# HGRN2's values and K turned by VectorE in 32x32 blocks and moved within SBUF, with the state products 25 steps later

## The chip, the cores and the metric

The kernel runs on one core of one Trainium2 chip. The metric is the device time of one execution in microseconds, the median of several runs; smaller is better. All times below come from those runs and from one execution recorded by the hardware profiler.

## The reference, cut to what matters

One inference step of one decoder layer for two groups of requests that share all weights: a prompt of 16 learned tokens and 256 tokens, and 8 samples of one token each, 280 columns in all. The layer is a half-step feed-forward network, a mixer, and a second feed-forward network, each with a layer norm. The mixer projects x to ten parts of 2048 columns and runs two recurrences beside each other, retention (8 heads of 256) and HGRN2 (16 heads of 128). The change is in HGRN2:

```
f = lb + (1.0 - lb) * sigmoid(f_h)          # forget gate, per channel
k = 1.0 - f
q = silu(q_h);  v = i_h
# per chunk, b = cumsum(log f):
o     = (A * v summed over j <= i) + (q * exp(b)) @ S
S_new = exp(b_last) * S + einsum('bhjd,bhjv->bhdv', k * exp(b_last - b), v)
```

The last line sums over the tokens j. On the chip the projections leave channels on the partitions and tokens along the row, so for this sum both the decayed K and v must be turned, so that tokens lie on the partitions. Outputs are the layer's result for both groups and the new states of both recurrences.

## The kernel before

**Products and weights.** Every projection runs in three passes on TensorE (PE), with weights and activations each split into a high and a low part (`dense`, L202; the products are L218). Weights come in units of eight 128x128 blocks. Each unit is loaded by a DMA on SP's queue (`raw`, L185), cast by ScalarE (ACT) to the high part (`whi`, L188), and VectorE (DVE) subtracts that for the low part (`wlo`, L189). Each of the three has three buffers, so the load of unit n+3 waits until `wlo` of unit n is made, and `whi` of unit n+3 waits until PE is through with unit n. 

**Groups.** The projection to ten parts is worked in groups of two outputs of 128 channels: for each unit u (a pair of HGRN2 heads and a retention head, 8 units) the groups f, q_h, i_h, q_r, k_r, v_r, then four gate groups of the unit before. In unit 0, f and q_h are one group, and so are i_h and q_r. A group has 16 k-steps, each of them six products (two weight blocks in three passes), so a steady unit has 160 k-steps. A group's two outputs take two of the four PSUM banks of the pool `ps_a`; the next group takes the other two, if they are free. The function `evacuate` (L643 on) reads them: f by a sigmoid and a scaling on ACT (L653, L654) and k = 1 - f (L655); q_h by a sigmoid on ACT (L660) and a multiplication on DVE (recorded at the helper's line L240); i_h by two ACT copies to v (L667, L668); q_r and k_r by the rotation on DVE (L677 to L680); v_r by ACT copies to the same tile v (L684, L686). The tiles f, k, v and vth have one buffer each.

**The mixers run between the k-steps.** `mix_hg` (HGRN2) and `mix_ret` (retention) are generators: after each k-step of a projection `pump` lets each run on to its next `yield n`, where n is the number of k-steps to wait. PE's order is the program's order. The orders on the other engines are made by the framework's scheduler before the run and are fixed as well; each engine works strictly in its order, and so does SP's queue of DMA issues.

**HGRN2's steps that the change touches.** Early in `mix_hg`, PE turns v by two transposes for each head (L875), ACT copies them to `vth` (L879), and POOL copies v's first and last tokens to `ends` (L750, L751). After the scan of decays, `turned(h)` turns K by two transposes for each head (L982) with an ACT copy to `kth` (L983). Later come the state products `pst` (km by vm for the learned tokens at L1022, then kth by vth at L1024), an ACT copy and two DVE steps to `Sh` (L1027), and its DMA out (L1030). After these, the samples' products `pq` (L1039) and the outputs follow. `load(1)` and `values(1)` fetch the second head's sample states; each first touches the tile by a small POOL copy of something that must be done before.

Unit 0 begins before the steady rhythm, unit 1 with other spacings; units 2 to 7 are called steady.

Of the kernel before, what the change touches and what calls it, by code (L numbers as in the profile page):

```python
# [18 lines left out]
P = 128  # L19
# [4 lines left out]
NMETA, SEQ, NS = 16, 256, 8  # L24
# [104 lines left out]
def trunk(ctx: ExitStack, tc: tile.TileContext, A, O):  # L129
# [417 lines left out]
    with tc.tile_pool(name="yp", bufs=1) as yp:  # L547
# [7 lines left out]
        with tc.tile_pool(name="mp", bufs=1) as mp:  # L555
# [73 lines left out]
            def project(groups):  # L629
                for grp in groups:  # L630

                    bank = mx_bank if grp[0] == (QKV_ORDER[2], 0) else acc_bank
                    outs = [bank(f"pj_{n}{c}") for n, c in grp]
                    x0s = [NMETA if n in LIVE else 0 for n, _ in grp]
                    if grp[0] == (QKV_ORDER[0], 0):
                        outs = norm1.first(block, outs, x0s)
                    elif grp[0] == (QKV_ORDER[2], 0):
                        v = st["i_h"] = tmp("v", (P, 2, T))
                        outs = norm1.second(block, outs, x0s, (v[:, 0, :], v[:, 1, :]))
# [71 lines left out]

            NB2 = LP - 2 * P
# [8 lines left out]
            def upper_upper_lower(out, x, at=0):  # L721
                n = x.shape[0]
                nc.scalar.copy(out[:n], x)
# [22 lines left out]
            def mix_hg(u, f, k, q, v):  # L746

                calm = 2
                ends = tmp("ends", (P, 2, 2, NMETA))
                nc.gpsimd.tensor_copy(ends[:, :, 0, :], v[:, :, :NMETA])  # L750
                nc.gpsimd.tensor_copy(ends[:, :, 1, :], v[:, :, T - NMETA :])  # L751
# [117 lines left out]
                vt = tmp("vth", (P, 2, 2, P))  # L869
                vrow = []  # L870
                for h in range(2):

                    pt = mx_bank("pt")
                    for b in range(2):
                        nc.tensor.transpose(pt[:, b * P : (b + 1) * P], v[:, h, NMETA + b * P : NMETA + (b + 1) * P], ident)  # L875
                    x = pt[:64, 2 * P : 3 * P]
                    if h:
                        nc.tensor.transpose(x, ends.rearrange("p c a t -> p (c a t)"), ident)
                    nc.scalar.copy(vt[:, h], pt[:, : 2 * P].rearrange("p (b f) -> p b f", b=2))  # L879
                    if h:  # L880
# [93 lines left out]
                kts = []  # L974

                def turned(h):
                    kt = tmp("kth", (P, 2, P), bufs=2)
                    kts.append(kt)
                    pt = mx_bank("ptk")
                    for b in range(2):  # L980
                        t0 = NMETA + b * P
                        nc.tensor.transpose(pt[:, b * P : (b + 1) * P], K[:, h, t0 : t0 + P], ident)  # L982
                    nc.scalar.copy(kt, pt[:, : 2 * P].rearrange("p (b f) -> p b f", b=2))  # L983
# [20 lines left out]
                turned(0)  # L1004
                load(1)
                yield 4
                turned(1)
# [5 lines left out]
                if u != 1:  # L1013
                    samples(1)
                    yield 4 if u == 0 else 5

                Ss = []
                for h in range(2):
# [4 lines left out]
                    for b in range(2):  # L1023
                        nc.tensor.matmul(pst[:, (b + 1) * P : (b + 2) * P], kts[h][:, b, :], vt[:, h, b, :], start=True, stop=True)  # L1024
# [9 lines left out]
                yield (8, 11, 45)[min(u, 2)]  # L1034
# [342 lines left out]
```

## Time and profile before

| what | value |
|---|---|
| device time, median of 3 runs | 2566.84 us |
| lowest and highest run | 2566.56 and 2567.51 us |
| span of the profiled execution | 2563.9 us |
| instructions in it | 56275 |
| VectorE, ScalarE busy | 66%, 54% |
| granted TensorE clock | nine tenths or more in all 40 slices |
| packets on the hardware DMA queue q1 | 156352 |

The span runs from the first to the last recorded instruction. No device time is listed for the profiled execution apart from the runs; its span lies 2.9 us below their median. The page also cuts the span into 40 equal slices of 64 us. The digit of each is the busy share in tenths: VectorE stands at 4 to 6 in the feed-forward networks and at 7 to 9 in the slices of the mixer, from about 770 us to 1850 us, and the DMA share alternates there between 6 and 7.

In rows of the timeline the first number is the start, the second the duration, then engine, line, operation, output and inputs. A bracket at a row's end says how long the engine stood idle before it, and what ended the wait.

### The profile page before, as it was taken

What the parts mean: (1) busy time and instruction counts of PE and PEld (TensorE: products, weight loads), DVE (VectorE), ACT (ScalarE), POOL (GpSimd) and SP (SyncE); (2) the same over time, 40 slices, a digit from 0 to 9 for tenths busy, and PEclk for the clock granted to TensorE, in tenths of its full rate; (3) what the DMA queues carried; (4) which work ended last, traced back from release to release, by engine and by line L of the source; (5) the groups of instructions that cost most, each with busy time, mean ns of one, the idle gap of its engine ahead of it and who ended that gap; (6) DMA issues with size and microseconds to landing.
All of it is one profiled execution on the core that took longest, in us unless ns stands there. A gap on an engine that the chain in (4) does not pass through costs nothing.

```text
span 2563.9 us, 56275 instructions
## 1 busy us (share of the span) xinstructions
PE 2553.4 (100%) x23424; PEld 2534.4 (99%) x23424; DVE 1702.8 (66%) x2827; ACT 1392.2 (54%) x2186; POOL 57.0 (2%) x152
## 2 busy tenths in 40 slices
PE   9999999999999999999999999999999999999999
PEld 9999999999999999999999999999999999999998
DVE  6444544475569878777777777777885555556555
ACT  5444444444456767767676666675564444444443
POOL 0000000000000000000000000000000000000000
PEclk9999999999999999999999999999999999999999
DMA  7555555555555876767676767675556565565554
GB/s 244 183 187 183 187 182 184 186 182 186 184 201 180 287 265 232 264 214 260 212 264 215 259 223 255 224 239 188 196 190 197 194 197 195 194 196 195 195 195 149
DMA packets 156897, 536.26 MB, mean 209 GB/s; under 512 B 17952, under 2 KB 25952, under 8 KB 156640
## 3 DMA queue, kind: packets, MB, share of 16 engines
q1 hardware_dynamic: 156352, 532.37, 62.0%
q8 instruction: 183, 3.00, 0.5%
q14 instruction: 74, 0.61, 0.1%
q10 hardware_dynamic: 288, 0.29, 0.0%
HBM read 501.99 MB, written 30.61 MB: 208 GB/s over the span
## 4 chain that ended last, share of the span: by engine, by line
PE 96%; DVE 2%; ACT 0%; issue 0%; DMA 0%; SPq 0%; ACTq 0%; DVEq 0%
PE up L218 36%; PE dn L218 19%; PE pj_i_h L218 3%; PE pj_g_r L218 3%; PE pj_q_h L218 3%; PE pj_g_h L218 3%; PE pj_a_r L218 3%; PE pj_a_h L218 3%; PE pj_f L218 3%; PE pj_q_r L218 3%; PE pj_k_r L218 3%; PE wo L218 3%; PE pj_v_r L218 3%; DVE wlo L189 1%; PE pqr L1211 1%; PE psr L1168 0%
## 5 line engine op out<-in xcount | busy, mean ns | idle before, releaser
L189 DVE TENSOR_TENSOR wlo<-raw,whi 128x1024 fp32r<-128x1024 f32 (+1 forms) x869 | 1062.2, 1223 | 740.7 <-ACT whi L188 737.3
L188 ACT CAST whi<-raw 128x1024 fp32r<-128x1024 f32 (+1 forms) x870 | 905.7, 1042 | 909.2 <-PE up L218 411.0
L218 PE MATMUL up<-xh,whi 128*128 128x280 f32 (+1 forms) x2624 | 725.6, 280 | 0.6 <-ACT whi L188 0.6
L218 PE MATMUL up<-xh,wlo 128*128 128x280 f32 (+1 forms) x2624 | 725.8, 280 | 0.4 <-DVE wlo L189 0.3
L218 PE MATMUL up<-xl,whi 128*128 128x280 f32 (+1 forms) x2624 | 725.4, 279 | 0.0
L218 PEld LDWEIGHTS up<-xh,wlo 128*128 128x128 f32 x2624 | 492.6, 189 | 1.0 <-DVE wlo L189 1.0
L218 PEld LDWEIGHTS up<-xh,whi 128*128 128x128 f32 x2624 | 492.6, 189 | 0.8 <-ACT whi L188 0.8
L218 PEld LDWEIGHTS up<-xl,whi 128*128 128x128 f32 x2624 | 492.6, 189 | 0.0
L218 PE MATMUL dn<-hh,whi 128*128 128x280 f32 (+1 forms) x1376 | 384.7, 280 | 0.0
L218 PE MATMUL dn<-hh,wlo 128*128 128x280 f32 (+1 forms) x1376 | 384.3, 279 | 0.0
L218 PE MATMUL dn<-hl,whi 128*128 128x280 f32 (+1 forms) x1376 | 384.3, 279 | 0.0
L218 PEld LDWEIGHTS dn<-hh,whi 128*128 128x128 f32 x1376 | 260.1, 189 | 0.1
L218 PEld LDWEIGHTS dn<-hl,whi 128*128 128x128 f32 x1376 | 260.1, 189 | 0.1
L218 PEld LDWEIGHTS dn<-hh,wlo 128*128 128x128 f32 x1376 | 260.1, 189 | 0.0
L218 PE MATMUL pj_k_r<-xh,whi 128*128 128x280 f32 x256 | 74.2, 290 | 0.0
L218 PE MATMUL pj_g_r<-xh,whi 128*128 128x264 f32 x256 | 74.0, 289 | 0.0
L218 PE MATMUL pj_v_r<-xh,whi 128*128 128x280 f32 x256 | 73.8, 288 | 0.0
L218 PE MATMUL pj_v_r<-xh,wlo 128*128 128x280 f32 x256 | 72.4, 283 | 0.3 <-DVE wlo L189 0.3
L218 PE MATMUL pj_g_h<-xh,whi 128*128 128x264 f32 x256 | 72.7, 284 | 0.0
L218 PE MATMUL pj_k_r<-xh,wlo 128*128 128x280 f32 x256 | 72.4, 283 | 0.0
L218 PE MATMUL pj_v_r<-xl,whi 128*128 128x280 f32 x256 | 72.3, 283 | 0.0
L218 PE MATMUL pj_k_r<-xl,whi 128*128 128x280 f32 x256 | 72.3, 283 | 0.0
(421 smaller groups left out, 5263.4 us busy)
## 6 DMA issues: line engine op xcount, KB each, us to landing
raw<-in_w_up SPq DMA_DIRECT2D x343, 512.0 KB, 4.1
raw<-in_w_in SPq DMA_DIRECT2D x320, 512.0 KB, 4.3
raw<-in_w_dn SPq DMA_DIRECT2D x172, 512.0 KB, 3.5
smr<-in_sr SPq DMA_DIRECT2D x32, 512.0 KB, 5.0
out_srs<-smr SPq DMA_DIRECT2D x32, 512.0 KB, 6.7
raw<-in_w_out SPq DMA_DIRECT2D x32, 512.0 KB, 3.9
vbr<-vrd SPq DMA_DIRECT2D x32, 256.0 KB, 4.1
smh<-in_sg SPq DMA_DIRECT2D x16, 512.0 KB, 5.2
```

The source lines that it names most:

```text
L188: nc.scalar.copy(hi[:, j:jn, :], raw[:, j:jn, :])
L189: nc.vector.tensor_tensor(out=lo[:, j0:j1, :], in0=raw[:, j0:j1, :], in1=hi[:, j0:j1, :].bitcast(F32), op=ALU.subtract)
L218: nc.tensor.matmul(o, w, t, start=start, stop=stop)
L1211: nc.tensor.matmul(pq[32 * j : 32 * j + 32, :256], qdr_at[c][:, 32 * b : 32 * b + 32], sms[2 * e + c][:, j, :], start=e + c == 0, stop=e + ...
```

## The change

PE's 64 transposes of v and K go, with the ACT copies behind them. In their place:

- VectorE's `transpose` turns each half of i_h straight from PSUM into a tile `z`, in 32x32 blocks: inside each block rows and columns are exchanged, but the blocks stay in their places. `z` lies in v's memory. In unit 0, i_h comes from two `rot` tiles instead of PSUM.
- The 16 blocks of each 128x128 are then brought to their places by DMAs from SBUF to SBUF (`turned_over`): one for each pair of a 32-partition source and a 32-partition target, 16 for v and 16 for K in each unit. A move takes 32 partitions with four runs of 32 numbers each, 16 KB. They are issued on SP's queue by a generator of their own, one each 2 k-steps, or each k-step for K in units 0 and 1.
- K is turned by one VectorE instruction into k's memory, and its moved blocks lie in f's memory. In the order's rows, moved K of unit 1 is called f_9917 and its unmoved blocks k_9918.
- `ends` is filled by four small ACT copies from i_h itself.
- The state products come later: in the steady units 30 instead of 5 steps after the second head's samples, in unit 0 8 instead of 4, and in unit 1 8 more. The wait after them is shorter by as much, so that what follows keeps its step.

```diff
@@ evacuate
                 elif n == "i_h":
-                    v = st.pop("i_h", None)
-                    if v is None:
-                        v = tmp("v", (P, 2, T))
-                        nc.scalar.copy(v[:, 0, :], o0)
-                        nc.scalar.copy(v[:, 1, :], o1)
-
-                    start(mix_hg(c0 // 2, st["f"], st["k"], st["q"], v), {0: 20, 2: 46}.get(c0, 4))
+                    ends = tmp("ends", (P, 2, 2, NMETA))
+                    vt = tmp("vth", TURNED)
+                    z = tmp("v", (P, 2, T)).rearrange("p h t -> p (h t)")[:, : 4 * P].rearrange("p (h b t) -> p h b t", h=2, b=2)
+                    for j, o in enumerate(st.pop("i_h", (o0, o1))):
+                        nc.vector.transpose(z[:, j].rearrange("p b t -> p (b t)"), o[:, NMETA:LP])
+                        nc.scalar.copy(ends[:, j, 0, :], o[:, :NMETA])
+                        nc.scalar.copy(ends[:, j, 1, :], o[:, T - NMETA : T])
+                    turned_over(vt, z, 2)
+                    start(mix_hg(c0 // 2, st["f"], st["k"], st["q"], ends, vt), {0: 20, 2: 46}.get(c0, 4))
...
+            def turned_over(out, z, pause):
+
+                def transfers():
+                    for i in range(0, P, 32):
+                        for j in range(0, P, 32):
+                            nc.sync.dma_start(out[j : j + 32, :, :, i : i + 32], z[i : i + 32, :, :, j : j + 32])
+                            yield pause
+
+                start(transfers(), 1)
@@ mix_hg
-                    nc.gpsimd.tensor_copy(sms[h][:, 0, :1], kts[0][:, 0, :1] if h else acc[:, 15:16])
+                    nc.gpsimd.tensor_copy(sms[h][:, 0, :1], k[:, 0, :1] if h else acc[:, 15:16])
...
-                    nc.gpsimd.tensor_copy(vbs[h][:, 0, :1], kts[1][:, 0, :1] if h else acc[:, 2 * P + 15 : 2 * P + 16])
+                    n = 32 if h else P
+                    nc.gpsimd.tensor_copy(vbs[h][:n, 0, :1], kt[:n, 0, 0, :1] if h else acc[:, 2 * P + 15 : 2 * P + 16])
...
-                    pt = mx_bank("pt")
-                    for b in range(2):
-                        nc.tensor.transpose(pt[:, b * P : (b + 1) * P], v[:, h, NMETA + b * P : NMETA + (b + 1) * P], ident)
-                    nc.scalar.copy(vt[:, h], pt[:, : 2 * P].rearrange("p (b f) -> p b f", b=2))
...
-                def turned(h):
-                    kt = tmp("kth", (P, 2, P), bufs=2)
-                    kts.append(kt)
-                    pt = mx_bank("ptk")
-                    for b in range(2):
-                        t0 = NMETA + b * P
-                        nc.tensor.transpose(pt[:, b * P : (b + 1) * P], K[:, h, t0 : t0 + P], ident)
-                    nc.scalar.copy(kt, pt[:, : 2 * P].rearrange("p (b f) -> p b f", b=2))
+                kt = f.rearrange("p h t -> p (h t)")[:, : 4 * P].rearrange("p (h b t) -> p h b t", h=2, b=2)
+
+                def turned():
+                    z = k.rearrange("p h t -> p (h t)")[:, : 4 * P].rearrange("p (h b t) -> p h b t", h=2, b=2)
+                    nc.vector.transpose(z.rearrange("p h b t -> p h (b t)"), K[:, :, NMETA:])
+                    turned_over(kt, z, 2 if steady else 1)
...
-                turned(0)
+                turned()
                 load(1)
                 yield 4
-                turned(1)
                 values(1)
...
                 if u != 1:
                     samples(1)
-                    yield 4 if u == 0 else 5
+                    yield 8 if u == 0 else 30
+                else:
+                    yield 8
...
-                        nc.tensor.matmul(pst[:, (b + 1) * P : (b + 2) * P], kts[h][:, b, :], vt[:, h, b, :], start=True, stop=True)
+                        nc.tensor.matmul(pst[:, (b + 1) * P : (b + 2) * P], kt[:, h, b], vt[:, h, b], start=True, stop=True)
...
-                yield (8, 11, 45)[min(u, 2)]
+                yield (4, 3, 20)[min(u, 2)]
```

Three places show how the change moves instructions. The first is PE at the end of q_h and the start of i_h of unit 1, before and after. `pj_q_h3` is the second bank of q_h, `pj_i_h2` and `pj_i_h3` are the two of i_h; the brackets name the semaphores that a product waits for.

```order
L218 MATMUL pj_q_h3_9910<-xh1_15_9295,wlo31_10043 128x264
L218 MATMUL pj_i_h2_10076<-xh1_0_9235,whi32_10079 128x280 [waits Activation_49]
L218 MATMUL pj_i_h2_10076<-xl1_0_9236,whi32_10079 128x280
L218 MATMUL pj_i_h2_10076<-xh1_0_9235,wlo32_10080 128x280 [waits DVE_49]
L218 MATMUL pj_i_h3_10077<-xh1_0_9235,whi32_10079 128x280 [waits PE_49]
L218 MATMUL pj_i_h3_10077<-xl1_0_9236,whi32_10079 128x280
```

```order
L218 MATMUL pj_q_h3_9925<-xh1_15_9296,wlo31_10058 128x264
L218 MATMUL pj_i_h2_10091<-xh1_0_9236,whi32_10094 128x280 [waits DVE_49]
L218 MATMUL pj_i_h2_10091<-xl1_0_9237,whi32_10094 128x280
L218 MATMUL pj_i_h2_10091<-xh1_0_9236,wlo32_10095 128x280
L218 MATMUL pj_i_h3_10092<-xh1_0_9236,whi32_10094 128x280 [waits DVE_49,PE_49]
L218 MATMUL pj_i_h3_10092<-xl1_0_9237,whi32_10094 128x280
```

Before, i_h's first product waited for ACT, the cast of its weights. Now both of its banks wait for DVE: they are the banks that q_h has just filled, and DVE's multiplication is their last reader.

The second is ACT: where f of unit 1 is evacuated (L653, from `pj_f2` and `pj_f3`), before and after. `sro` belongs to retention of unit 0, `kept` to HGRN2's scan in unit 0, `smh` to the samples of unit 0, and `Sh` to its state products.

```order
L1170 COPY sro_9862<-psr_9854 128x256
L918 COPY kept_9712<-K_9497 128x256
L1170 COPY sro_9887<-psr_9879 128x256
L653 ACTIVATE f_9902<-pj_f2_9626 128x280
L188 CAST whi30_9978<-raw30_9977 128x8x128
L654 ACTIVATE f_9902<-f_9902,lb_85,olb_86 128x280
L653 ACTIVATE f_9902<-pj_f3_9627 128x280
```

```order
L225 CAST rhi_10507<-sqr_10502 128x264
L188 CAST whi42_10667<-raw42_10666 128x8x128
L999 ACTIVATE smh_10266<-smh_10266,meta_8644 128x128 x3
L188 CAST whi43_10718<-raw43_10717 128x8x128
L1027 COPY Sh_10622<-pst_10623 128x128
L653 ACTIVATE f_9917<-pj_f2_9641 128x280
L653 ACTIVATE f_9917<-pj_f3_9642 128x280
L654 ACTIVATE f_9917<-f_9917,lb_85,olb_86 128x280 x2
L1027 COPY Sh_10631<-pst_10632 128x128
```

Before, f was evacuated beside the cast of weight unit 30, the third unit of q_h. Now it stands behind the cast of unit 43, the last of k_r, and behind the first state product of unit 0, whose K lies in f's memory.

The third is SP's queue around the weight load `raw74`, before and after. Weight units 68 to 71 are q_h of unit 2, in which unit 1's state products now stand.

```order
L185 DMA raw71_12123<-in_w_in 128x1024
L185 DMA raw72_12175<-in_w_in 128x1024
L1002 DMA out_sgs<-smh_11457 128x1024
L1030 DMA out_sgp<-Sh_11945 128x128
L1030 DMA out_sgp<-Sh_11954 128x128
L185 DMA raw73_12205<-in_w_in 128x1024
L1002 DMA out_sgs<-smh_11715 128x1024
L185 DMA raw74_12235<-in_w_in 128x1024
```

```order
L185 DMA raw71_12163<-in_w_in 128x1024
L735 DMA f_9917<-k_9918 32x4x32 x5
L185 DMA raw72_12215<-in_w_in 128x1024
L735 DMA f_9917<-k_9918 32x4x32
L1003 DMA out_sgs<-smh_11490 128x1024
L185 DMA raw73_12245<-in_w_in 128x1024
L735 DMA f_9917<-k_9918 32x4x32 x2
L185 DMA raw74_12275<-in_w_in 128x1024
L735 DMA f_9917<-k_9918 32x4x32 x2
```

Before, the queue held only weight loads and outputs here. Now the last ten moves of unit 1's K stand between them, the last two behind `raw74`.

More of the change, by code (lines that the diff above doesn't have):

```diff
@@ L637, in project @@
                     elif grp[0] == (QKV_ORDER[2], 0):
-                        v = st["i_h"] = tmp("v", (P, 2, T))
-                        outs = norm1.second(block, outs, x0s, (v[:, 0, :], v[:, 1, :]))
+                        first = st["i_h"] = [tmp("rot") for _ in range(2)]
+                        outs = norm1.second(block, outs, x0s, first)
                     else:
@@ L710, in evacuate @@
                             split(yh[c0], yl[c0], y)
+            TURNED = (P, 2, 2, P)
             NB2 = LP - 2 * P
@@ L744, in sample_columns, with mix_hg @@
                     po[:, 3 * P :].rearrange("p (j c) -> p c j", c=32)[:, : 2 * n, :].rearrange("p (h e) j -> p h e j", e=2))
-            def mix_hg(u, f, k, q, v):
+            def mix_hg(u, f, k, q, ends, vt):
                 calm = 2
-                ends = tmp("ends", (P, 2, 2, NMETA))
-                nc.gpsimd.tensor_copy(ends[:, :, 0, :], v[:, :, :NMETA])
-                nc.gpsimd.tensor_copy(ends[:, :, 1, :], v[:, :, T - NMETA :])
                 Q = tmp("Q", (P, 2, SEQ))
@@ L868, in mix_hg @@
                 Q1 = side_by_side(1)
-                vt = tmp("vth", (P, 2, 2, P))
                 vrow = []
                 for h in range(2):
-                    pt = mx_bank("pt")
-                    for b in range(2):
-                        nc.tensor.transpose(pt[:, b * P : (b + 1) * P], v[:, h, NMETA + b * P : NMETA + (b + 1) * P], ident)
-                    x = pt[:64, 2 * P : 3 * P]
                     if h:
+                        x = mx_bank("pt")[:64, :P]
                         nc.tensor.transpose(x, ends.rearrange("p c a t -> p (c a t)"), ident)
-                    nc.scalar.copy(vt[:, h], pt[:, : 2 * P].rearrange("p (b f) -> p b f", b=2))
-                    if h:
                         nc.scalar.copy(vsm[:64], x)
@@ L973, in mix_hg @@
                 on_h[u] = on
-                kts = []
-                def turned(h):
-                    kt = tmp("kth", (P, 2, P), bufs=2)
-                    kts.append(kt)
-                    pt = mx_bank("ptk")
-                    for b in range(2):
-                        t0 = NMETA + b * P
-                        nc.tensor.transpose(pt[:, b * P : (b + 1) * P], K[:, h, t0 : t0 + P], ident)
-                    nc.scalar.copy(kt, pt[:, : 2 * P].rearrange("p (b f) -> p b f", b=2))
+                kt = f.rearrange("p h t -> p (h t)")[:, : 4 * P].rearrange("p (h b t) -> p h b t", h=2, b=2)
[3 more added lines that the diff above has]
+                    turned_over(kt, z, 2 if steady else 1)
                 def gate():
```

2 rows, old and new, of the table rows are left out of this document.

## The prediction

> **What bounds the kernel now.** I read the page first: span and busy times, and the chain that ended last.
>
> ```profile
> span 2563.9 us, 56275 instructions
> PE 2553.4 (100%) x23424; PEld 2534.4 (99%) x23424; DVE 1702.8 (66%) x2827; ACT 1392.2 (54%) x2186; POOL 57.0 (2%) x152
> PE 96%; DVE 2%; ACT 0%; issue 0%; DMA 0%; SPq 0%; ACTq 0%; DVEq 0%
> ```
>
> TensorE is busy from end to end and 96% of the chain is its own work. A PE instruction that goes shortens the span, and a PE wait that comes lengthens it, microsecond for microsecond; what happens on the other engines counts only where PE comes to wait for it. Then the windows (length, then busy time and count of PE, PE loads, DVE, ACT, POOL; clock, DMA share, GB/s): one steady unit of HGRN2 (one of eight pairs of heads), ten microseconds in the second unit, and the whole stretch that the change touches.
>
> ```profile
> 1190.72:1317.05 126.33, 126.33 (x1278) 124.66 (x1282) 98.73 (x195) 84.97 (x158) 6.18 (x14) 1.00 0.71 240
> 870.00:880.00 10.00, 10.00 (x88) 10.00 (x87) 9.85 (x27) 9.28 (x22) 0.00 (x0) 1.00 1.00 389
> 780.00:1800.00 1020.00, 1017.56 (x10235) 1001.67 (x10234) 815.59 (x1638) 686.38 (x1290) 55.05 (x128) 1.00 0.70 237
> ```
>
> A steady unit has VectorE at 78% and the DMA engines at 0.71: room for more. The second unit has none: at 870 to 880 VectorE is 98.5% and ScalarE 93% busy and the DMA share is 1.00, because unit 0's late work, the samples of two units and the next unit's first work fall together there. PE doesn't wait for them there today only because its accumulators alternate between two pairs of PSUM banks. The case turns on that place.
>
> **What goes from PE.** Timeline of one pair of v transposes between two projection products (start, duration, engine, line, operation), and the two transposed tiles (count; least, median, most ns):
>
> ```profile
> 1627.31 0.28 PE L218 MATMUL pj_q_r<-xh,wlo 128*128 128x264 f32 x1
> 1627.42 0.38 PE L875 MATMUL pt<-ident,v 128*128 128x128 f32 x2
> 1627.56 0.36 PE L218 MATMUL pj_q_r<-xh,whi 128*128 128x264 f32 x1
> 1627.76 0.28 PE L218 MATMUL pj_q_r<-xl,whi 128*128 128x264 f32 x1
> ```
>
> ```profile
> L875 PE MATMUL pt<-ident,v x32: 272/273/273, 805.3 to 1628.4; 128*128 128x128 f32 x32
> L982 PE MATMUL ptk<-ident,K x32: 272/273/273, 853.6 to 1648.7; 128*128 128x128 f32 x32
> ```
>
> The 272 ns of one are pipeline length, not cost. Products follow each other every 0.11 us, so without the pair the last two rows would start at 1627.42 and 1627.53; they start at 1627.56 and 1627.76. The delay that stays is 0.23 us, say 0.22. There are 64 transposes, 32 pairs: 32 x 0.22 = 7.1 us. Unit 0's two v pairs (0.44 us) stand in a stretch where PE waits for weights anyway and give nothing: 6.7 us is the gain. The ACT and POOL copies that go too are on engines that aren't the bound in steady units.
>
> **What is added, and where it is covered.** The trace has no 32x32 transpose. The nearest rows are VectorE operations on one operand of 128x280, on two of 128x512, and one on PSUM:
>
> ```profile
> L412 DVE TENSOR_SCALAR v<-ls,wgb x2: 353/353/353, 796.6 to 797.6; 128x280 f32<-128x280 f32 x2
> 803.23 0.68 DVE L240 TENSOR_TENSOR Q<-q,f 128x512 f32<-128x512 f32 x1
> 847.39 0.42 DVE L240 TENSOR_TENSOR q<-q,pj_q_h 128x264 f32<-128x264 f32 x1
> ```
>
> I take 0.35 for a v half (0.42 at most, by the PSUM row; not under 0.3, since both move as many elements) and 0.68 for K. Per unit that is 1.4 us against 27.6 idle in a steady unit: covered; were it not, it would cost at most 1.4 x 6. The Trainium skill, "VectorE: DVE Perf Modes", section "The three transpose paths", gives 390 ns for a 128x128 bf16 transpose on TensorE and 311 on VectorE, and its "Rules for kernel authors" say to use TensorE where PSUM will do, which speaks against this change. Read as an estimate, 311 ns for each 128 columns would make the units' VectorE work 20 us rather than 11, and unit 0 below 0.6 us dearer; no run here shows it yet, and the 0.22 us of the PE rows is well under its 390.
>
> The moves are 32 DMAs a unit, 256 in all, each 32 partitions x 4 runs of 128 B = 16 KB, all on SP's queue, which issues one in about 0.33 us and spends half of its time waiting for a weight buffer:
>
> ```profile
> SPq L185 <- DVE wlo L189: 1294.1, 577, 3.8
> 815.57 0.33 SPq L185 DMA_DIRECT2D raw<-in_w_in  x1
> q1 hardware_dynamic: 156352, 532.37, 62.0%
> ```
>
> SP's share is 32 x 0.33 = 10.6 us a unit, inside those waits. On the DMA engines the two bounds lie far apart. By bytes: 256 x 16 KB = 4.2 MB at the 389 GB/s of the window above is 11 us of 1020, share 0.70 to 0.71. By packets: 62.0% x 16 x 2563.9 / 156352 = 0.163 us for a mean packet, and 32,768 runs at that are 334 us of sixteen engines, share 0.70 to 1.03. A packet of 128 B carries a twenty-seventh of the mean 3.4 KB, so I take the end by bytes, doubled for its packets: no cost. The Trainium skill, "DMA: Bandwidth & Descriptors", has rules for both ends: "Rules for kernel authors" calls transfers under 64 KB mostly overhead, "Why small descriptors are slow (HBM only)" exempts transfers within SBUF. The second agrees with my choice; the first is the rival of the full queue.
>
> In the steady units 2 to 7 the order has a unit's K in place some four weight units (16 steps) ahead of the state products, which is what the 25 steps bought; banks alternate as before; I find no new PE wait. Units 0 and 1 are otherwise, in five places.
>
> **A, unit 0's v (+3.2).** PE waits here for the weights' low part:
>
> ```profile
> 815.60 0.39 PE L218 MATMUL pj_f<-xh,wlo 128*128 128x280 f32 x1 [0.73 <-DVE wlo L189]
> 817.29 0.39 ACT L684 COPY v<-pj_v_r 128x280 f32<-128x280 f32 x1
> 817.73 0.33 PE L1107 MATMUL pt<-ident,v 128*128 128x128 f32 x1
> ```
>
> Two transposes ahead of such weights delay PE by 0.7. And retention's v is copied by ACT into the tile from which the 16 moves of HGRN2's v read, so the copy waits for the last of them; PE's retention transposes (L1107) wait for the copy at 817.73. On SP the last two moves stand behind the weight load of 815.57, so they go out by 816.6. How long a small move within SBUF takes no row shows; other small transfers:
>
> ```profile
> out_srp<-sro SPq DMA_DIRECT2D x16, 128.0 KB, 2.3
> ...
> out_sgp<-Sh SPq DMA_DIRECT2D x16, 64.0 KB, 4.8
> ```
>
> 2.3 to 4.8 us give 818.9 to 821.4 against the copy's 817.29: 1.6 to 4.1, 2.5 taken.
>
> **B, q_h to i_h of unit 1 (+5.1).** K turned now lies in f's memory. The next f's evacuation (ACT, L653) therefore waits for unit 0's 16 moves of K and its state products, which read them, in k_r(1). Until then two of the four accumulator banks are held, and q_h, i_h, q_r and k_r of unit 1 all run in the other two, each waiting for the group before it to be read.
>
> ```profile
> 844.26 0.28 PE L218 MATMUL pj_i_h<-xh,whi 128*128 128x280 f32 x1
> 844.61 0.28 PE L218 MATMUL pj_i_h<-xh,whi 128*128 128x280 f32 x1
> ...
> 849.27 0.42 DVE L240 TENSOR_TENSOR q<-q,pj_q_h 128x264 f32<-128x264 f32 x1
> ```
>
> i_h's second product began at 844.61; VectorE read q_h's second bank until 849.27 + 0.42 = 849.69. PE waits 5.1 us: 3.5 if ACT, without f's evacuations and the copies of K, runs ahead; 6 with the two sample updates that the order now has ahead of that row.
>
> **C, i_h to q_r (+1.8).** q_r may begin when i_h's banks are read: two transposes at 0.35, or the weight cast that stands on ACT at that point, then the copies of the ends.
>
> ```profile
> 862.30 0.20 ACT L723 CAST sc<-scr 16x16 fp32r<-16x16 f32 x1 [0.78 <-DVE scr L240]
> 863.03 1.05 ACT L188 CAST whi<-raw 128x1024 fp32r<-128x1024 f32 x1
> ```
>
> 1.05 + 4 x 0.20 = 1.85; 1 to 3.
>
> **D, q_r to k_r (+4.9).** The rotation (VectorE) reads q_r's banks, behind the backlog of the window 870 to 880:
>
> ```profile
> 872.35 0.28 PE L218 MATMUL pj_k_r<-xh,whi 128*128 128x280 f32 x1
> 877.17 0.43 DVE L677 SCALAR_TENSOR_TENSOR q_r<-pj_q_r,sin 128x264 f32<-128x264 f32 x1
> ```
>
> 877.60 - 872.35 = 5.25, less some 0.3 for two small copies of f and k that the order moved behind: 4.9; 3 if the engines catch up during B, 6 if C's work pushes them.
>
> **E, unit 1's state products (+6.0).** They now stand in q_h(2), two k-steps into its second weight unit, and wait for the last two moves of K, which on SP stand behind a weight load.
>
> ```profile
> 967.01 2.02 PE pj_q_h L218 x18
> 969.03 0.23 PE pvr L237 x2
> 969.26 5.40 PE pj_q_h L218 x48
> ```
>
> ```profile
> 974.19 1.22 DVE L189 TENSOR_TENSOR wlo<-raw,whi 128x1024 fp32r<-128x1024 f32 x1 [0.25 <-issue]
> ...
> 975.44 0.34 SPq L185 DMA_DIRECT2D raw<-in_w_in  x1
> ```
>
> By those rows the products would start at 969.26 + 18/48 x 5.40 = 971.3, 36 matmuls into q_h. That load went at 975.44, since ACT and VectorE were behind; work that moves out ahead of it makes it some 2 us earlier, 973.5. Two issues of 0.33 and 2.3 to 4.8 of landing: 976.5 to 979, a wait of 5.2 to 7.7; 3.4 to 9.7 with the load's time left open. I take 6.0.
>
> **The sum.** -6.7 + 3.2 + 5.1 + 1.8 + 4.9 + 6.0 = +14.3. The profiled span is 2563.9, 2.9 us under the median of the runs, 2566.84, and I take this difference to stay: 2566.84 + 14.3 = **2581**. All low ends together (2.3 + 3.5 + 1 + 3 + 3.4 = 13.2) give 2573, all high ends (4.8 + 6 + 3 + 6 + 9.7 = 29.5) 2590.
>
> **The rivals.**
>
> Covered after all (faster): the copies of f and the moves of K(0) end so early that the banks come free as before, and A and E land in time. For it: 96% of the chain is PE's own work, so today almost nothing is late. Against it: f's evacuation stands on ACT behind the copy of the first state products, an order that no speed changes. 2566.8 - 6.7 = 2560. Chance 0.13.
>
> The engines catch up (no change): the stalls of B, C and D aren't three but one backlog; while PE stands, VectorE works it off and the next wait is short, and E's load comes earlier for the same reason. For it, the window between B and D:
>
> ```profile
> 855.00:860.00 5.00, 5.00 (x50) 4.80 (x52) 2.76 (x4) 4.06 (x13) 2.26 (x3) 1.00 0.94 289
> ```
>
> VectorE has 2.24 us free there. Against it: in 870 to 880, where D's rows lie, it has 0.15. Half of 21.0 - 6.7 = +3.8, 2570.6. Chance 0.18.
>
> Each steady unit waits too (slower): moves spaced two steps apart with one weight load between are late by as much as E's 2 to 4 us in six units: 2581 + 6 x 3 = 2599. It decides if a move takes longer than 16 steps (11 us) to land; against it stand 2.3 to 4.8. Chance 0.08.
>
> The DMA queue fills (slower): packets at 0.163 us, share 1.03, is 0.03 x 1020 = 30 us more: 2611. It decides if a 128 B packet costs more than 0.15 us; against it, the window at 389 GB/s with share 1.00. Chance 0.05.
>
> That the change doesn't do what it says is excluded: the 64 PE instructions are gone from the order.
>
> **How the numbers follow.** Forecast 0.56, the rivals 0.13, 0.18, 0.08 and 0.05. 0.2% is 5.1 us, about what a measurement of this kernel can tell from no change: 2561.7 to 2572.0 is the same. So faster 0.13, same 0.18, slower 0.69. The forecast's own range is 2573 to 2590; the range to hold 8 in 10 takes in the second rival with its spread down to 2564 and the third up to 2600.
>
> **What would show it.** PE's waits in the changed trace: i_h(1) for the q multiplications of some 5 us, q_r(1) for ScalarE's ends, k_r(1) for the rotation, pst in q_h(2) for a DMA, the retention transposes of unit 0 for v. No PE wait in the six steady units, whose length falls by 4 x 0.22 = 0.9 us from 126.33. A 32x32 transpose at 0.35 and 0.68. DMA share in 780 to 1800 at most 0.75. It is wrong if i_h(1) starts without a wait (the banks), if the pst wait is under 1 us (the load), or if steady units grow.

## The result, and the profile after

The changed kernel takes 2601.45 us (median of 4 runs, 2598.13 to 2605.07) against 2566.7 before: a ratio of 1.0136, interval 1.0121 to 1.0150. It is 34.8 us slower where 14.3 were forecast: 11.5 us above the forecast's own range (2573 to 2590) and 1.5 above the wide one (2564 to 2600). The span of the profiled execution lies 1.9 us above the median of the runs, that of before 2.9 below, so the traces stand 39.4 apart; what follows accounts for these.

The page of the changed kernel: span, busy times, chain, and the packets of the DMA queue.

```profile
span 2603.3 us, 56474 instructions
PE 2560.0 (98%) x23360; PEld 2536.8 (97%) x23360; DVE 1712.3 (66%) x2851; ACT 1382.8 (53%) x2172; POOL 44.6 (2%) x136
...
q1 hardware_dynamic: 193216, 536.58, 64.2%
...
PE 85%; DVE 6%; DMA 4%; ACT 3%; issue 1%; SPq 0%; POOL 0%; ACTq 0%; DVEq 0%
```

VectorE's busy time rose by 9.5 us and is still two thirds of the span; the queue's share rose by two hundredths. The new thing is in the chain, where TensorE's own work fell from 96% to 85%. What it waits for, in the view of waits (total, times, longest):

```profile
PE pst L1026 <- DMA out_sgs<-smh: 9.5, 1, 9.5
PE pj_k_r L218 <- DVE q_r L679: 5.2, 1, 5.2
PE pj_i_h L218 <- DVE q L240: 5.0, 2, 3.7
PE pt L1109 <- ACT v L686: 4.8, 4, 2.9
PE pt L1118 <- POOL tails L1105: 4.5, 5, 1.0
PE pj_g_h L218 <- ACT v L686: 2.7, 1, 2.7
PE pj_q_r L218 <- ACT ends L670: 1.3, 1, 1.3
```

These are the five forecast places and two that were not: `pj_g_h`, and the retention's transposes in steady units (all five waits for `tails`, three of the four for v). The DMA named in the first row only shares a semaphore with the one awaited: the products read the moves of K, as a later row shows.

These seven rows make 33.0 us, less 0.9 for `tails` that the kernel before had too; 6.7 of TensorE's work should go besides, so some 13 of the 39.4 are not in them. Most of that shows in windows of the changed kernel, in the column before the last two, the granted TensorE clock:

```profile
850.00:860.00 10.00, 7.93 (x131) 7.20 (x132) 6.95 (x18) 2.65 (x9) 0.56 (x3) 0.66 0.85 265
880.00:890.00 10.00, 4.75 (x39) 4.59 (x38) 9.58 (x28) 7.03 (x19) 0.00 (x0) 0.89 0.73 239
890.00:900.00 10.00, 10.00 (x68) 10.00 (x68) 2.73 (x7) 3.87 (x8) 0.00 (x0) 0.77 0.57 209
990.00:1000.00 10.00, 1.83 (x17) 1.68 (x15) 7.36 (x19) 6.13 (x13) 0.00 (x0) 0.85 0.81 261
1000.00:1010.00 10.00, 8.65 (x73) 8.36 (x74) 3.56 (x11) 5.74 (x11) 0.00 (x0) 0.64 0.57 186
```

From 890 to 900 TensorE is busy all the time and does 68 products, where a full window of ten microseconds in the kernel before held 88 (870 to 880, above). A clock of 0.66 over 10 us is 6.8 us at half speed; the two next rows together give 2.2 + 4.6 = 6.8, the last two 3.0 + 7.2 = 10.2. Each stretch begins in one of the three longest waits, those of 3.7, 5.2 and 9.5. Less the part in which TensorE stood anyway, i_h lost 2.5, k_r 2.8 and q_h of unit 2 3.0 us: 8.2 us that no wait shows. 33.0 - 0.9 + 8.2 - 6.7 = 33.6; of the 5.8 us left, 0.6 arose ahead of the mixer; the rest I can't place by rows. The Trainium skill, "TensorE: Matmul & The Clock Gate", section "Part 1: The HAM clock gate (the "warmup" mystery)", says that the clock falls to half after an idle window of about 3.4 us and comes back after a busy one, in windows that run free; the stretches here are two, two and three times 3.41 us, so the trace agrees on the windows. It doesn't agree that a whole window must be idle: less was enough in these runs (last section).

A steady unit, from f's first product in unit 3 to that in unit 4, has grown from 126.33 to 127.45 us:

```profile
1120.15:1247.60 127.45, 126.16 (x1268) 123.87 (x1267) 99.47 (x198) 83.05 (x156) 4.37 (x12) 1.00 0.74 241
```

### The profile page after: what moved, and what is told of

The parts are those of the page before. It is cut to its first block, busy times and chain, and to the rows that moved or that the text cites. A ratio compares the mean times of both kernels' runs of the same rounds, so it can differ in the third digit from the quotient of the medians.

```text
span 2603.3 us, 56474 instructions
## 1 busy us (share of the span) xinstructions
PE 2560.0 (98%) x23360; PEld 2536.8 (97%) x23360; DVE 1712.3 (66%) x2851; ACT 1382.8 (53%) x2172; POOL 44.6 (2%) x136
## 3 DMA queue, kind: packets, MB, share of 16 engines
q1 hardware_dynamic: 193216, 536.58, 64.2%
## 4 chain that ended last, share of the span: by engine, by line
PE 85%; DVE 6%; DMA 4%; ACT 3%; issue 1%; SPq 0%; POOL 0%; ACTq 0%; DVEq 0%
PE up L218 35%; PE dn L218 18%; PE pj_i_h L218 3%; PE wo L218 3%; PE pj_q_h L218 3%; PE pj_q_r L218 3%; PE pj_f L218 3%; PE pj_g_h L218 3%; PE pj_a_h L218 3%; PE pj_g_r L218 2%; PE pj_a_r L218 2%; DVE wlo L189 2%; PE pj_k_r L218 2%; ACT whi L188 1%; DMA raw<-in_w_in 1%
```

## The experiments

Theory 1: the time went into single waits, which come from buffers that K and v now share with the next user, and into the half clock behind the long ones. Theory 2, the rival: VectorE and the DMA queue are full in the dense units, and a wait that is taken away comes back elsewhere. Theory 3 came after the first four runs: the moves end late, because SP issues them in order between weight loads. Medians stand beside 2566.7 to 2567.6 of the kernel before in the same runs. The table has, for the profiled executions, how much later than before a group's first product began (timelines; all include up to 1.1 us that arose ahead of the change).

| first product of | changed | k0_own | k1_pool | one_dma | k0_one | fill2 | steady |
|---|---|---|---|---|---|---|---|
| q_h, unit 1 | 2.6 | 2.9 | 2.3 | 2.5 | 4.3 | 3.0 | 0.1 |
| i_h, unit 1 | 6.5 | 2.9 | 6.3 | 6.2 | 4.3 | 5.9 | 0.1 |
| q_r, unit 1 | 11.2 | 2.5 | 11.0 | 11.1 | 3.8 | 9.0 | 0.1 |
| k_r, unit 1 | 16.7 | 2.5 | 16.5 | 16.6 | 3.8 | 14.5 | 0.0 |
| v_r, unit 1 | 19.5 | 16.3 | 19.2 | 19.5 | 6.1 | 14.6 | 0.0 |
| i_h, unit 2 | 34.2 | 28.3 | 22.4 | 22.2 | 7.2 | 25.4 | 0.7 |
| f, unit 3 | 34.7 | 28.6 | 23.2 | 23.1 | 9.9 | 24.8 | 4.8 |
| f, unit 7 | 39.9 | 31.2 | 25.5 | 21.3 | 7.3 | 29.2 | 7.8 |
| output projection | 39.4 | 30.2 | 25.4 | 20.9 | 7.4 | 31.1 | 7.8 |

**k0_own: unit 0's moved K in a free buffer.**

```diff
+                home = f if u else tmp("on_h", (P, 2, TL), bufs=2)
-                kt = f.rearrange(...)
+                kt = home.rearrange(...)
```

> Unit 0's moved K lies in a free buffer instead of f's memory; nothing else changes. Theory 1 (the time went into single waits, and into TensorE's halved clock after those of over some 3.5 us): i_h, q_r and k_r of unit 1 no longer wait (3.7 + 1.3 + 1.3 + 5.25 us) and the two stretches of half clock behind them (2.5 + 2.8 us of loss) go: 2601.5 - 16.9 = about 2585. Theory 2 (the added work of VectorE and the DMA queue in the dense second unit is what costs; a wait that is taken away comes back at the next place): less than half of that, 2594 or more, with new TensorE waits in unit 1.

2596.2 us (1.0113, interval 1.0098 to 1.0128), the time that was named for Theory 2. The three waits are gone: k_r begins 2.5 us late instead of 16.7. But the state products of unit 0 now wait in k_r. The largest waits of this run:

```profile
PE pst L1027 <- DMA out_sgs<-smh: 9.7, 1, 9.7
PE pst L1027 <- DMA f<-k: 8.2, 1, 8.2
```

The first is unit 0's, the second unit 1's. So f's memory was the cause of the three waits, as Theory 1 says, and yet little was gained: the moves of unit 0's K end at nearly the same time as in the changed kernel (SP was through with issuing them at 885.3 us there, at 887.8 here), and what waited ahead of them there had hidden that. This gave Theory 3.

**values_k: another source for the small copy that holds a load back.**

```diff
-                    n = 32 if h else P
-                    nc.gpsimd.tensor_copy(vbs[h][:n, 0, :1], kt[:n, 0, 0, :1] if h else ...)
+                    nc.gpsimd.tensor_copy(vbs[h][:, 0, :1], k[:, 0, :1] if h else ...)
```

> The small copy that holds back the load of the second head's sample values waits for the turned K alone, no longer for the first of its moves. Theory 1: SP's queue is no longer blocked for some 5 us a unit behind that load, weights come in time, and the steady units' TensorE waits (0.3 to 1.0 for v and 0.95 for the tails, 6 us in all) go: 2595 to 2597. Theory 2 (these waits come from the moves themselves being slow and filling the queue): no change, 2601.

2600.1 (1.0132, 1.0117 to 1.0147): inside the spread of the changed kernel, and not the gain of Theory 1. The waits for `tails` (4.5) and v (4.4) stay.

**v_pause1: v's moves one each step.**

```diff
-                    turned_over(vt, z, 2)
+                    turned_over(vt, z, 1)
```

> The moves of v are issued one each k-step instead of one each two. Theory 1: unit 0's wait for v (2.9 us) goes, since its moves are through 16 steps earlier; unit 1's wait of 2.7 stays, since its moves can't start before unit 0's outputs have read the single buffer: 2598 to 2599. Theory 2 (the queue is full): the weight loads that the denser moves stand before come later, and the time rises to 2604 or more.

2602.7 (1.0138, 1.0123 to 1.0153): no gain. Unit 0's wait for v fell from 2.9 to 2.0, but its wait for `tails` (0.9) came back, and the steady units kept theirs.

**k1_pool: unit 1's moves of K issued by GpSimd.**

```diff
-                    turned_over(kt, z, 2 if steady else 1)
+                    turned_over(kt, z, 2 if steady else 1, nc.gpsimd if u == 1 else nc.sync)
```

> Unit 1's moves of K are issued by GpSimd instead of SP; all others stay on SP. Theory 1: unit 1's state products waited 9.5 us because the last moves stood on SP behind weight loads that wait for VectorE. Free of these they land in time, and the wait and the half clock behind it (3 us) go: 2601.5 - 12.5 = 2589, or part of it if GpSimd takes over 1 us for each. Theory 2 (the moves themselves take that long to land): no change.

2591.5 (1.0095, 1.0078 to 1.0112), 10 us less. The wait of unit 1's state products is gone with the half clock behind it: i_h of unit 2 begins 22.4 us late instead of 34.2. The rows of DMA issues (KB, median us to landing) show what a move takes:

```profile
f<-k SPq DMA_DIRECT2D x112, 16.0 KB
f<-k POOLq DMA_DIRECT2D x16, 16.0 KB, 6.0
```

6.0 us from issue to landing, for 16 KB inside SBUF, and still in time: it was SP's order that was late. In the changed kernel SP's rows ahead of the products read:

```profile
993.66 1.77 SPq L735 DMA_DIRECT2D f<-k  x2
995.74 0.36 SPq L185 DMA_DIRECT2D raw<-in_w_in  x1
996.14 1.24 SPq L735 DMA_DIRECT2D f<-k  x2
...
1001.35 0.55 PE L1026 MATMUL pst<-vth,f 128*128 128x128 f32 x1 [9.52 <-DMA out_sgs<-smh]
```

The last two moves go out behind that weight load, by 997.4, land 4.0 us later, and the product starts.

**k0_kpool and k0_allpool: both mended, and GpSimd for K's moves or for all.** Both take k0_own's edit, and `nc.gpsimd` in place of `nc.sync` for K in all units, the second for v too.

> Unit 0's moved K in the free buffer, and all moves of K issued by GpSimd; v's moves stay on SP. Theory 3 (formed after the first runs: the moves end late because they are issued in order with the weight loads on SP at 0.6 us each; a buffer freed elsewhere only shows the next wait for them): with both mended, the waits of i_h, q_r and k_r of unit 1, the 9.7 us of unit 0's state products that then showed, the 9.5 of unit 1's, and all half clock go: 2601.5 - 16.9 - 12.5 = about 2572, and the steady units' 6 us shrink too, to 2568 to 2572. Theory 2 (the queue and VectorE are full): new waits come up in unit 1, and it stays at 2585 or more.

> As the last, and v's moves are issued by GpSimd too, so SP issues none. Theory 3: also the waits for v (2.9 in unit 0, 2.7 in unit 1) and the rest of the steady units' go, since weight loads no longer stand behind moves: 2601.5 - 36.5 = 2562 to 2567, level with the kernel before or below it. Theory 2, or GpSimd's queue becoming what SP's was: 2570 or more, with waits for the tails that GpSimd copies.

2616.3 (1.0193, 1.0178 to 1.0208) and 2610.7 (1.0168, 1.0153 to 1.0184): slower than the changed kernel. Up to i_h of unit 2 they are 20 us ahead of it (13.9 and 13.5 late instead of 34.2). The rest is lost again in the steady units, at waits for weights that grow to 3.7 us, most of them followed by 3.4 or 6.8 us at half clock:

```profile
PE pj_g_r L218 <- ACT whi L188: 16.6, 6, 3.7
PE por L1229 <- ACT sc L727: 9.2, 1, 9.2
```

GpSimd's small copies now stand behind its moves, and SP's loads that they release stand behind them: in k0_kpool SP waits 27.9 us for `vbh`. That the weights are late because they stand behind these loads is argued from the order, and no run shows it alone. The 9.2 us in unit 1 come from the next shared buffer. ScalarE's row there:

```profile
875.17 0.67 ACT L655 ACTIVATE k<-f 128x560 f32<-128x560 f32 x1 [11.34 <-DMA on_h<-k]
```

The moves of unit 0's K read from k's memory, and the next k can't be written until the last has read.

**fill and fill2: dummy products in the waits.** Products of a constant with itself into an unused bank, ahead of i_h and k_r of unit 1 and of unit 1's state products; they leave no results.

```diff
+                    fill_pe({("i_h", 2): 13, ("k_r", 2): 20}.get(grp[0], 0))     # fill: 26, 38
+                fill_pe(36 if u == 1 else 0)                                        # fill: 66
```

> As the changed kernel, with dummy products on TensorE ahead of three of its waits in units 1 and 2 (26 of them before i_h, 38 before k_r, 66 before unit 1's state products), shorter than the waits; they leave no results. If the half clock comes from TensorE standing idle, it stays at full speed there and the time falls by up to 8.2 us, to 2593 to 2596, with the engines' waits at the same places. If the half clock has another cause (power, the matmuls after it), nothing falls, or it rises: 2601 to 2605.

> The dummy products again at half the number (13, 20 and 36), since one takes 0.22 us and the first try was longer than the waits that it should fill. Theory: no half clock behind those three waits, each product still starting when its releaser allows: 2601.5 - 8.2 = 2593. If the clock doesn't matter: 2601.

fill took 2604.2 (1.0145, 1.0130 to 1.0160), which by its number alone would speak for another cause, but it was mis-sized: a product took 0.23 us, so the fillings of 6.0, 8.7 and 14.9 us were longer than the waits. fill2 took 2596.5 (1.0112, 1.0098 to 1.0126), 4.9 less than the changed kernel by the medians, with intervals that overlap a little. The span of its profiled execution, 2595.1, is 8.2 under that of the changed kernel; since that one was the longest of its four, it is in part luck that this equals the 8.2 worked out above. The table shows the gain where the half clock was: from i_h to q_r of unit 1, 4.7 us become 3.1, from k_r to v_r 2.8 become 0.1. The windows of fill2 in which the changed kernel had the half clock:

```profile
850.00:860.00 10.00, 8.27 (x152) 7.80 (x152) 7.31 (x18) 3.24 (x10) 0.96 (x3) 1.00 0.94 307
890.00:900.00 10.00, 10.00 (x109) 9.66 (x109) 7.21 (x22) 8.62 (x16) 0.00 (x0) 1.00 0.58 198
1000.00:1010.00 10.00, 10.00 (x111) 9.80 (x111) 8.59 (x28) 7.68 (x16) 0.21 (x1) 1.00 0.41 124
```

The clock is 1.00 in all three, though the products still start only when what they wait for is there. So it was idleness that took the clock away.

**one_dma and k0_one: one dense DMA instead of 16 moves.** The first in the changed kernel, the second with k0_own's edit. The blocks stay in their unturned places, so this is no version to use.

```diff
-                    for i in range(0, P, 32):
-                        for j in range(0, P, 32):
-                            nc.sync.dma_start(out[j : j + 32, :, :, i : i + 32], z[i : i + 32, :, :, j : j + 32])
-                            yield pause
+                    nc.sync.dma_start(out, z)
+                    yield pause
```

> Each set of 16 moves is replaced by one dense DMA of the same 256 KB between the same two buffers; the blocks are then left in their unturned places, so products with them use other numbers. Buffers and the waits on them are unchanged. Theory 3: the waits for late moves go (v's 2.9 and 2.7, the state products' 9.5, the steady units' 6), the waits from f's memory (i_h, q_r, k_r: 11.5 and 5.3 of half clock) stay at first, 2601.5 - 23 = about 2578. Theory 1 without 3 (the shared buffers alone): 2590 or more. If the transposes on VectorE were the cost: 2600.

> Unit 0's moved K in the free buffer, and each 16 moves replaced by one dense DMA (the blocks then stay unturned, so products with them use other numbers). Theory 3: the only kernel with neither f's memory in the way nor late moves; the 16.9 us of unit 1 go in addition to the dense DMA's 2584.7: 2566 to 2569. Theory 2: k0_own gave 5 us, so 2580.

2584.7 (1.0065, 1.0048 to 1.0082) and 2571.3 (1.0014, 1.0006 to 1.0023), each some us above what Theory 3 had named and under its rivals. With the same bytes and buffers in one issue, unit 1's state products don't wait and the steady units gain 0.44 us each (from 23.1 to 21.3 between f of unit 3 and of unit 7), while i_h, q_r and k_r wait as before; with f's memory free too, those go as well. The waits of one_dma, then of k0_one:

```profile
PE pj_k_r L218 <- DVE q_r L679: 5.2, 1, 5.2
PE pj_i_h L218 <- DVE q L240: 4.8, 2, 3.6
```

```profile
PE pt L1117 <- POOL tails L1104: 2.3, 4, 1.0
PE pt L1108 <- ACT v L686: 2.2, 2, 2.0
PE pj_g_r L218 <- DVE wlo L189: 1.6, 1, 1.6
```

All of VectorE's new transposes are in both. Theory 2 is thereby refuted for VectorE; the shared memory and the 16 moves carry most of the loss. What k0_one keeps, 3.7 us over the kernel before and some 10 over one that had the gain of 6.7 alone, is more than the waits shown, and isn't resolved.

**steady, steady_later and steady_values: units 0 and 1 as before.** TensorE turns v and K in units 0 and 1 by the old code, the new path runs in units 2 to 7. steady_later also takes values_k's edit and starts retention's mixing 7 steps after v_r instead of 3; steady_values takes values_k's edit alone.

> Units 0 and 1 as in the kernel before (TensorE turns v and K there); units 2 to 7 as in the changed kernel. Theory 3: the loss of units 0 and 1 goes whole. What stays are six units with 0.88 us less of TensorE's work and waits of 0.95 to 1.9 each at retention's transposes: 2566.8 - 5.3 + 6 to 8 = 2567 to 2570. Theory 2 (the moves' load as such): a loss that grows with the units, some 10 us or more, 2577.

> As the last, with two more edits in the steady units: the copy that holds back the second head's sample values waits for the turned K alone, and retention's mixing starts 7 steps after v_r instead of 3, so that its transposes come 2.8 us later than ScalarE's copy of v, which is some 2 us late there. Theory 3: the waits of the steady units go and 6 x 0.88 us stay as gain: 2566.8 - 5.3 = about 2561.5. Theory 2: waits turn up at the weights instead, 2566 or more.

> Units 0 and 1 as in the kernel before; in units 2 to 7 only the copy for the second head's sample values is changed, the moves stay on SP and retention's mixing starts as in the changed kernel. It parts the two edits of the slower run of 2586: if the later start of the mixing did the harm, this one is at 2571 to 2575; if the edit of the copy did it, 2582 or more.

2575.4 (1.0032, 1.0020 to 1.0045), 2586.4 (1.0070, 1.0056 to 1.0084) and 2571.9 (1.0017, 1.0008 to 1.0026). Of the 34.8 us, 26 go with units 0 and 1. But the six steady units lose 7.8 us by themselves, 1.3 each in the mean, unevenly: 4.1 of it lie between i_h of unit 2 and f of unit 3. That is nearer to Theory 2's 2577 than to Theory 3's 2567 to 2570. ScalarE's wait for weight loads, in the kernel before and in steady:

```profile
ACT whi L188 <- DMA raw<-in_w_in: 40.7, 27, 3.1
```

```profile
ACT whi L188 <- DMA raw<-in_w_in: 59.1, 30, 3.5
```

Weights come later, ScalarE's copy of v with them, and TensorE's retention transposes wait. That these waits would go if the transposes started later was wrong: steady_later turned them into more waits, for weights.

```profile
PE pj_g_r L218 <- DVE wlo L189: 12.0, 11, 2.4
```

steady_values, which differs from steady_later in that alone, shows that the later start did the harm. That the edit of the copy helps a little isn't shown: the intervals of steady_values and steady overlap.

**steady_pool: the last, with GpSimd as issuer.**

> Units 0 and 1 as in the kernel before; in units 2 to 7 all moves are issued by GpSimd, and the copy that holds back the second head's sample values waits for the turned K alone. SP then issues what it issued before. Theory A (the steady units lose because 32 issues of 0.6 us each stand on SP between the weight loads): the 6 x 0.88 us of gain show, 2561.5 to 2564, below the kernel before. Theory B (the moves' packets slow the weight loads on the DMA engines, whoever issues them): as in the run with SP, 2573 to 2577, with ScalarE waiting for weights as there.

2590.1 (1.0088, 1.0074 to 1.0101): neither theory's number. SP was free of moves and ScalarE's wait for weight loads fell to 46.2 us, but GpSimd's own small copies came late behind its moves. VectorE's wait for one of them is new:

```profile
DVE smh L1032 <- POOL meta L1023: 21.2, 6, 4.4
```

So the last question stays open: whether a steady unit loses by SP's time of issue or by the moves' packets. That one dense DMA of the same bytes turns a loss into a gain fits both. One figure of the traces leans to the issue: from unit 3 to unit 7 the 4 KB packets of the loads took 195.9 ns in the mean in the changed kernel and as long in k0_one, whose steady units gain; but the time that a packet waits for its turn isn't in it. No version that computes the whole beat the kernel before; steady_values came nearest.

## Why the prediction was wrong

**Gain, 6.7 forecast.** Right where it can be seen alone. In the steady units k_r begins 0.44 us earlier, measured from q_r, where the two pairs of v were, and v_r 0.44 earlier, measured from k_r, where the two pairs of K were: 0.88 a unit, as forecast.

**VectorE's price.** Two rows of the changed kernel, median and mean ns of one:

```profile
L668 DVE STREAM_TRANSPOSE v<-pj_i_h x14: 407/438/450, 867.2 to 1665.1; 128x256 f32<-128x256 f32 x14
```

```profile
L983 DVE STREAM_TRANSPOSE k<-K 128x512 f32<-128x512 f32 x8 | 5.7, 708 | 0.0
```

0.44 and 0.71 where 0.35 and 0.68 stood; nothing hangs on it. **The moves' packets.** In the changed kernel's trace a packet of 128 B took 13 ns (median of all of that size). 32,768 of them are 27 us of sixteen engines, near the 22 that were taken (11 by bytes, doubled) and far from the 334 by packets. The queue's time grew by more, 64.2% x 2603.3 - 62.0% x 2563.9 = 82 us, mostly because the 4 KB packets took 201 ns in the mean instead of 194. The share in the stretch that the change touches rose from 0.70 to 0.72: the queue did not fill.

**A.** 2.9 of waiting for v, of which 0.9 stood in the `tails` wait that it hides: 2.1 net against 3.2. The 0.7 for two transposes ahead of late weights didn't come: that wait is 0.5, where it was 0.7 before. **B, C, D.** 5.0, 1.3 and 5.2 against 5.1, 1.8 and 4.9. Places and sizes were right, and the second rival's thought that the three were one backlog was wrong. **E.** 9.5 against 6.0, at the top of its bounds (3.4 to 9.7). It was mis-sized in the weight load, which didn't come 2 us earlier (it went 3.9 us after the products were due; the rows of before gave 4.1), and in 0.33 us for an issue; the moves' rows on SP say 0.6:

```profile
L735 SPq DMA_DIRECT2D f<-k x128: 585/599/1559, 867.3 to 1710.2; - x128
```

**The step that failed** is the sum itself, in two terms that it lacks. First, each wait was costed at its own length. TensorE at rest loses its clock, and three of the five waits were long enough, and 8.2 us went there that no wait shows; fill2 shows that idleness is the cause. The rule stands in the Trainium skill ("TensorE: Matmul & The Clock Gate", "Why this matters for your kernels": no idle gaps of over some 3 us), and no row of before could show it, since TensorE there never stood for more than 1 us. Second, "in the steady units I find no new PE wait". I had tested whether the moves end before their readers, not what stands behind them on SP. The unit above is 2.0 us (0.88 + 1.12) longer than forecast; over the last five steady units the trace has +4.7 where I had -4.4. What stands in place of "no new wait" is ScalarE's longer wait for weight loads and TensorE's waits at retention's transposes (6.3 us in the steady units of the changed kernel, none before); that the 32 issues of 0.6 us on SP are the cause, and not the moves' packets, is argued and stays open. A further 2.7 us, `pj_g_h`, are A's mechanism in unit 1, where v's moves can't begin until unit 0's outputs have read the one vth buffer; I had followed it in unit 0 alone.

The second rival (engines catch up) failed at its premise: VectorE did work off its backlog during B, but its rows ahead of the rotation hang on inputs that come after i_h (in 870 to 880 of the changed kernel it stood 3.4 us for a product of TensorE, `pqr`). The third rival (each steady unit waits too) came near the measured time, 2599, and that was luck: the steady units gave about half of its 18 us, and the half clock, which it didn't have, much of the rest. Its mechanism was another too: it said that K's moves come late for their reader; it was the weights that came late.

## What to carry to other kernels

A wait of a kernel that keeps TensorE busy costs its length and, where it is long, work after it at half speed (always here from 3.5 us on, and sometimes from 2 us on); cost the two apart. Where an instruction that reads locally is replaced by transfers that read a buffer for longer, list every next writer of each buffer, source and target: here f, k, v and vth each gave a wait, and taking the first away showed the next. And many small DMAs in the queue that feeds the weights can delay the weights, even where their bytes and their own readers are covered (ScalarE's wait for weight loads: 40.7 us before, 59.1 in steady, 46.2 with GpSimd as issuer); moving them to an idle engine's queue puts them ahead of that engine's own small work.

## What the runs showed of the hardware that was not expected

- A move inside SBUF of 32 partitions x 4 runs of 128 B held SP's queue for 0.60 us, against 0.33 for a weight load of 512 KB, and took 3.6 to 6.0 us to land when GpSimd issued it (medians of k0_allpool and k1_pool). The Trainium skill, "DMA: Bandwidth & Descriptors", "Rules for kernel authors", calls transfers under 64 KB mostly overhead; the issue and the landing agree with that. The Trainium skill, "DMA: Bandwidth & Descriptors", "Why small descriptors are slow (HBM only)", exempts transfers within SBUF from the penalty of small pieces; here 128 B took 13 ns and 4 KB 159 (medians), so the small packets moved bytes at some 0.4 of the rate.
- Waits of 3.7, 5.2 and 9.5 us were followed by 6.8, 6.8 and 10.2 us at half clock, those of 2.7 and 2.9 of the same execution by none; in k0_own's execution the same 2.9 was followed by 3.4 us of it, and in fill's one of 2.2. What decides is not the length of a wait but how much of it falls into one window of 3.41 us. In each execution all half clock begins on one grid of that step. The two windows around the wait of 2.9 us (816 to 823), in the changed kernel and then in k0_own (second number: TensorE busy):

```profile
816.07:819.48 3.41, 1.97 (x16) 1.76 (x15) 2.52 (x6) 1.98 (x5) 0.00 (x0) 1.00 0.52 163
819.48:822.89 3.41, 1.91 (x16) 1.91 (x17) 2.08 (x3) 3.12 (x7) 0.57 (x1) 1.00 0.54 165
```

```profile
816.70:820.11 3.41, 0.74 (x7) 0.53 (x5) 2.15 (x4) 2.06 (x5) 0.00 (x0) 1.00 0.67 197
820.11:823.52 3.41, 3.14 (x14) 3.14 (x15) 1.65 (x3) 2.51 (x6) 0.57 (x1) 0.50 0.51 198
```

In the first the grid cuts the wait into 1.4 and 1.5 us, and the clock stays; in the second 2.7 us fall into one window, and the next is at half clock. Thirteen of the traces have half clock in the mixer, 40 stretches. Each began right behind a window in which TensorE had stood 1.91 us or more, and no other window at full clock in these traces had more than 1.77. The grid is taken from the stretches themselves and the ends of products are modelled, so the limit is approximate.
